# One decoder layer on one core, its instructions put in order by the framework's timeline simulator

## The chip, the core and the metric

The kernel runs on one core of a Trainium2 chip. A core has five engines that work side by side, each through its own list of instructions in a fixed order: TensorE (PE) multiplies matrices and writes PSUM; VectorE (DVE), ScalarE (ACT) and GpSimd (POOL) work on elements; SyncE (SP) here only issues transfers. The engines wait for each other through semaphores. The metric is the device time of one execution in microseconds (us).

## The reference

The layer works on 1024 tokens with 1024 features, all in float32. It is a SwiGLU half step, a mixer of three parallel branches, and a second SwiGLU half step, each between two RMS norms:

```python
f1 = swiglu(rms_norm(h, ffn1_pre_g), ffn1_w_in, ffn1_w_out)      # width 2816
h = h + 0.5 * rms_norm(f1, ffn1_post_g)
u = rms_norm(h, mix_pre_g)
p_rwkv, p_swa, q_mem, gate_logits = split(u @ w_in)
y_a = rwkv7_mix(p_rwkv, ...)              # recurrence over the tokens, 8 heads of 64
y_b = sliding_window_gqa_sinks(...)       # window of 128, 8 query and 2 key heads
y_c = memory_cross_attention(q_mem, ...)  # 256 memory tokens, 4 heads of 128
g_a, g_b, g_c = split(sigmoid(gate_logits + gate_b))
merged = g_a * (y_a @ w_branch[0]) + g_b * (y_b @ w_branch[1]) + g_c * (y_c @ w_branch[2])
h = h + rms_norm(merged @ w_out, mix_post_g)
f2 = swiglu(rms_norm(h, ffn2_pre_g), ffn2_w_in, ffn2_w_out)
h = h + 0.5 * rms_norm(f2, ffn2_post_g)
```

## The kernel before

Features lie on the 128 partitions, tokens along the free axis, in halves of 512. Each large product is made of three matmuls (`mm3`, lines 354 to 356): a value is kept as a rounded part and a remainder (`w_hi`, `w_lo` of a weight; `u` and the like of an input), and the product of the two remainders is left out. A weight tile of 128x512 is loaded by SP into one of 5 buffers `w_raw` (line 269), rounded by ACT into `w_hi` (line 278), and DVE writes the remainder `w_lo` (line 280). There are 8 buffers (`OPS`) for such pairs, so that the pairs are made ahead of the matmuls that use them. Inputs are split in the same way (lines 462 and 463). Both feed-forward stages use a scheme of block products with fewer multiplications, whose sums and differences DVE makes; their parts pass through DRAM (`form_d`, `first_d`, `ffn_sum_d`), stored and loaded by SP (lines 674, 750, 650).

The stages, in order of time: the start (memory keys and values), the first feed-forward stage (to about 700 us), the preparation of the recurrence (`rwkv_prep`, four head pairs, to about 900), the inversion of small triangular matrices on DVE (`rwkv_invert`), beside which PE makes projections, the recurrence in 16 chunks of 64 tokens (`rwkv_chain`, about 1050 to 1155), its norm (`rwkv_finish`), the attention in 16 blocks (`attention`, to about 1460; 8 `MemoryBlock`, 8 `WindowBlock`), the last branch (`last_branches`, to about 1540), the output projection and the second feed-forward stage.

One chunk of the recurrence is a line of small matmuls between which DVE works: `z` (matmul, then a copy, line 1209), its product with the inverse (then two copies to `uv`, line 1218), the new state (a product, then `ts`, line 1227, and `sv`, line 1229), on which the next chunk's `z` waits. Beside it DVE masks the next chunk's gram matrices (`gz`, line 1171), and POOL scales the old state (`sw`, line 1212). Matmuls of two gate projections (`pgate`) are traced behind the chain for PE to use in its waits.

A window block computes scores into PSUM (`sc`, line 94), which ACT and DVE read (lines 127, 128), takes a softmax (line 132 to 142, eight normalisations on line 142), turns the result by PE (`ptr`, line 97), and empties that PSUM bank by ACT (line 152) and DVE (`pt`, line 155). Four PSUM banks serve such tiles (tag `bg`), four others the main products (tag `mm`). In the last branch the gated product is added to the sum by POOL (line 1555).

What sets the order: the Python code is traced once, instruction by instruction, inside a `TileContext`. When the context closes, the framework gives each engine its order. It walks through a simulated execution; where an engine is free, it takes that engine's ready instruction of highest priority. Priority is the traced order, moved forward in blocks under `high_priority(offset=...)` (300 for the weight stream, 1000 for urgent work). Two calls bind the order whatever the simulation says: `keep_in_program_order` puts an instruction behind the one traced before it on its engine (all small matmuls of the recurrence and the attention, and the loads of the start), and `issue_after` puts a group behind a named instruction. For example, the filling of the attention with gate and branch matmuls:

```python
def fill(self, n, behind):
    self.missing += n
    with self.tc.issue_after(behind.ins):
        while self.missing > 0:
            self.missing -= next(self.fills, n)
```

The large matmuls themselves, most of the work of DVE and ACT, and SP's transfers behind the start are free to be placed by the simulated times. The semaphore waits follow from the data and from the order.

Of the kernel before, what the change touches and what calls it, by code (L numbers as in the profile page):

```python
# [1835 lines left out]
def make(arrays):  # L1836
    nc = bacc.Bacc("TRN2", target_bir_lowering=False, num_devices=1, dynamic_dma_scratch_size=SCRATCH)
    io = {}
    for name, a in arrays.items():
        io[name] = nc.dram_tensor(f"in_{name}", a.shape, mybir.dt.from_np(a.dtype), kind="ExternalInput").ap()  # L1840
    io["out"] = nc.dram_tensor("out", [P, KD, T], F32, kind="ExternalOutput").ap()
    with tile.TileContext(nc) as tc:
        Builder(nc, tc, io).build()
    return nc

# [7 lines left out]
```

## Time and profile before

| what | value |
|---|---|
| time, median of 3 runs | 2271.61 us (2271.33 to 2272.18) |
| profiled execution | 2273.16 us |
| its span, first to last instruction | 2271.1 us |
| PE busy | 2244.2 us, 99% of the span |
| weight loads of PE | 1842.2 us, 81% |
| DVE, ACT, POOL busy | 1644.5, 997.3, 80.6 us |
| mean granted PE clock | 0.997 |
| DMA traffic | 417.66 MB, 184 GB/s |

The page of the profile gives busy times, the chain of work that ended last and the costliest groups. A group's row reads: line of the code, engine, operation, output and inputs by their names in the program, shapes, count, busy time, mean duration in ns, and the idle time of the engine before these instructions with what ended it. The waits view has rows of the form "engine, line, waited for: total us, times, longest us". The timeline has the start, the length, the engine and the instruction, with the idle time before it in brackets. SPq and ACTq are the transfers that SP and ACT issue. The granted clock is a share of full speed.

### The profile page before, as it was taken

The page shows a single profiled execution, that of the slowest core. Times are in us where ns is not written, and L with a number is a line of the kernel's source. Part 1 is how long each engine was busy: PE and PEld are TensorE (multiplying, and loading weights), DVE is VectorE, ACT ScalarE, POOL GpSimd, SP SyncE. Part 2 cuts the span into 40 slices and gives each one's busy share as a digit, 9 for nine tenths or more (in the row PEclk, how much of TensorE's full clock was granted, in tenths as well). Part 3 has the DMA queues.
Part 4 walks back from the last instruction along what each step waited for, and adds up shares of the span by engine and source line. Part 5 has one row for each costly group of instructions (what it writes and reads, how often), then busy time and mean ns, then how long its engine had stood idle before and what let it go on. Part 6 is the DMA issues. An engine that isn't in the chain of part 4 may idle for free.

```text
span 2271.1 us, 33412 instructions
## 1 busy us (share of the span) xinstructions
PE 2244.2 (99%) x11868; PEld 1842.2 (81%) x11868; DVE 1644.5 (72%) x2700; ACT 997.3 (44%) x1877; POOL 80.6 (4%) x130
## 2 busy tenths in 40 slices
PE   8999999999999999999999999999999999999998
PEld 6888888888888788888878887778888888888887
DVE  6987767666698885995666576665898885656676
ACT  6533333454555653123444454335663233345451
POOL 0000000000000000001320000031000000000000
PEclk9999999999999999999999999999999999999999
DMA  8465666686654467225438885554465652347763
GB/s 290 156 209 167 219 210 214 209 275 203 193 164 153 116 148 194 105 97 192 146 117 264 289 272 167 201 165 150 158 228 176 193 174 93 114 159 244 216 195 121
DMA packets 280775, 417.66 MB, mean 184 GB/s; under 512 B 82304, under 2 KB 104320, under 8 KB 280352
## 3 DMA queue, kind: packets, MB, share of 16 engines
q1 hardware_dynamic: 272832, 400.26, 55.4%
q10 hardware_dynamic: 7776, 15.28, 2.0%
q8 instruction: 93, 1.52, 0.3%
q14 instruction: 74, 0.61, 0.1%
HBM read 284.89 MB, written 129.50 MB: 182 GB/s over the span
## 4 chain that ended last, share of the span: by engine, by line
PE 90%; DVE 5%; ACT 1%; issue 1%; DMA 1%; POOL 1%; ACTq 0%; SPq 0%; DVEq 0%; POOLq 0%
PE px L354 7%; PE px L356 7%; PE px L355 7%; PE po L355 6%; PE po L354 6%; PE po L356 6%; PE pgate L354 4%; PE pgate L355 4%; PE pgate L356 4%; PE pz L355 3%; PE pz L354 3%; PE pz L356 3%; PE pr L354 2%; PE pr L355 2%; PE pr L356 2%; PE pq L355 1%
## 5 line engine op out<-in xcount | busy, mean ns | idle before, releaser
L278 ACT CAST w_hi<-w_raw 128x512 fp32r<-128x512 f32 x594 | 367.2, 620 | 694.6 <-PE px L355 160.1
L280 DVE TENSOR_TENSOR w_lo<-w_raw,w_hi 128x512 fp32r<-128x512 f32 x594 | 409.2, 690 | 189.2 <-ACT w_hi L278 168.1
L354 PE MATMUL po<-u,w_hi 128*128 128x512 f32 (+1 forms) x476 | 180.9, 380 | 0.0
L356 PE MATMUL po<-u,w_lo 128*128 128x512 f32 (+1 forms) x476 | 180.9, 380 | 0.0
L355 PE MATMUL po<-u,w_hi 128*128 128x512 f32 (+1 forms) x476 | 180.9, 380 | 0.0
L354 PE MATMUL pgate<-u,w_hi 128*128 128x512 f32 x384 | 154.9, 403 | 0.0
L356 PE MATMUL pgate<-u,w_lo 128*128 128x512 f32 x384 | 151.5, 395 | 0.0
L355 PE MATMUL pgate<-u,w_hi 128*128 128x512 f32 x384 | 149.8, 390 | 0.0
L355 PE MATMUL px<-f,w_hi 128*128 128x512 f32 x352 | 137.1, 389 | 0.9 <-DVE f L463 0.9
L354 PE MATMUL px<-u,w_hi 128*128 128x512 f32 x352 | 137.1, 389 | 0.8 <-DVE km L1424 0.8
L354 PE MATMUL px<-f,w_hi 128*128 128x512 f32 x352 | 137.1, 389 | 0.0
L356 PE MATMUL px<-u,w_lo 128*128 128x512 f32 x352 | 137.0, 389 | 0.0
L356 PE MATMUL px<-f,w_lo 128*128 128x512 f32 x352 | 137.0, 389 | 0.0
L355 PE MATMUL px<-u,w_hi 128*128 128x512 f32 x352 | 137.0, 389 | 0.0
L356 PE MATMUL pz<-u,w_lo 128*128 128x512 f32 x352 | 136.9, 389 | 0.0
L354 PE MATMUL pz<-u,w_hi 128*128 128x512 f32 x352 | 136.9, 389 | 0.0
L355 PE MATMUL pz<-u,w_hi 128*128 128x512 f32 x352 | 136.9, 389 | 0.0
L463 DVE TENSOR_TENSOR u<-hid,u 128x512 fp32r<-128x512 f32 x114 | 78.2, 689 | 45.9 <-ACT u L462 45.0
L354 PEld LDWEIGHTS po<-u,w_hi 128*128 128x128 f32 x476 | 89.5, 188 | 17.1
L355 PEld LDWEIGHTS po<-u,w_hi 128*128 128x128 f32 x476 | 89.5, 188 | 17.1
L356 PEld LDWEIGHTS po<-u,w_lo 128*128 128x128 f32 x476 | 89.5, 188 | 16.8
L462 ACT CAST u<-hid 128x512 fp32r<-128x512 f32 x114 | 70.7, 620 | 64.3 <-DMA hid<-form_d 55.1
(397 smaller groups left out, 5111.2 us busy)
## 6 DMA issues: line engine op xcount, KB each, us to landing
w_raw<-in_ffn_in SPq DMA_DIRECT2D x220, 256.0 KB
hid<-form_d SPq DMA_DIRECT2D x154, 256.0 KB
w_raw<-in_win SPq DMA_DIRECT2D x112, 256.0 KB
form_d<-g SPq DMA_DIRECT2D x88, 256.0 KB
w_raw<-ffn_sum_d SPq DMA_DIRECT2D x88, 256.0 KB
form_d<-h SPq DMA_DIRECT2D x66, 256.0 KB
w_raw<-in_ffn_out SPq DMA_DIRECT2D x66, 256.0 KB
gate_d<-gate SPq DMA_DIRECT2D x24, 512.0 KB
```

Of the source, the lines that this page charges most:

```text
L278: self.nc.scalar.copy(hi, x)
L280: self.split_last = self.nc.vector.tensor_tensor(lo, x, hi.bitcast(F32), ALU.subtract)
L354: mm(out, wh, xh, start=first, stop=False, **kw)
L355: mm(out, wh, xl, start=False, stop=False, **kw)
L356: self.last_mm = mm(out, wl, xh, start=False, stop=last, **kw)
L462: self.nc.scalar.copy(hi, x)
L463: self.nc.vector.tensor_tensor(lo, x, hi.bitcast(F32), ALU.subtract)
```

## The change

The context in which the program is traced gets one argument. The framework then walks through the execution with another simulator, which it calls its timeline simulator, when it chooses the order. The traced instructions, their sizes, the buffers, the priorities and the bound orders are the same.

```diff
-    with tile.TileContext(nc) as tc:
+    with tile.TileContext(nc, schedule_with_timeline_sim=True) as tc:
         Builder(nc, tc, io).build()
     return nc
```

## The prediction

> **What bounds the kernel now.** I read the page first: the span, the shares of the engines, and the chain of work that ended last.
>
> ```profile
> span 2271.1 us, 33412 instructions
> ...
> PE 2244.2 (99%) x11868; PEld 1842.2 (81%) x11868; DVE 1644.5 (72%) x2700; ACT 997.3 (44%) x1877; POOL 80.6 (4%) x130
> ...
> PE 90%; DVE 5%; ACT 1%; issue 1%; DMA 1%; POOL 1%; ACTq 0%; SPq 0%; DVEq 0%; POOLq 0%
> ```
>
> TensorE (PE) is busy for 2244.2 of 2271.1 us, and 90% of the chain is its own work. Its idle time is 26.9 us. The change adds and removes no operation, so PE's work stays what it is, and the time can only move through PE's holes: fewer than 26.9 us of them, or more. So the second view is the windows view, cut by stage, which says where the holes are (columns after the window: its length, then busy time and count of PE, weight loads, DVE, ACT, POOL, then granted clock, DMA share and GB/s).
>
> ```profile
> 0.00:20.00 20.00, 13.57 (x53) 11.66 (x54) 9.32 (x20) 12.92 (x22) 0.70 (x6) 1.00 0.91 344
> 100.00:700.00 600.00, 599.96 (x2645) 495.57 (x2644) 445.61 (x722) 258.27 (x443) 2.82 (x15) 1.00 0.63 204
> 700.00:900.00 200.00, 197.82 (x1094) 159.07 (x1093) 163.01 (x188) 107.86 (x167) 4.01 (x16) 1.00 0.55 138
> 900.00:1050.00 150.00, 150.00 (x685) 124.13 (x685) 122.06 (x153) 33.98 (x58) 1.58 (x4) 1.00 0.41 145
> 1050.00:1156.00 106.00, 104.69 (x1915) 87.30 (x1913) 65.13 (x163) 44.40 (x106) 35.08 (x60) 1.00 0.43 128
> 1156.00:1200.00 44.00, 42.95 (x173) 31.89 (x172) 25.17 (x36) 20.10 (x30) 8.50 (x9) 1.00 0.46 156
> 1200.00:1376.00 176.00, 176.00 (x946) 146.74 (x945) 120.17 (x257) 88.11 (x245) 0.96 (x1) 1.00 0.83 272
> 1376.00:1392.00 16.00, 14.70 (x52) 10.68 (x51) 10.21 (x27) 9.21 (x34) 0.00 (x0) 0.79 0.56 186
> 1460.00:1540.00 80.00, 77.52 (x340) 63.24 (x339) 53.48 (x78) 24.11 (x42) 20.68 (x14) 1.00 0.54 179
> 1540.00:2060.00 520.00, 519.64 (x2288) 428.47 (x2286) 382.73 (x607) 226.72 (x395) 3.27 (x2) 1.00 0.50 164
> 2240.00:2271.00 31.00, 21.31 (x176) 20.95 (x175) 17.63 (x49) 5.84 (x16) 2.95 (x4) 0.88 0.33 103
> ```
>
> The two feed-forward stages (100 to 700, 1540 to 2060) have 0.04 and 0.36 us of holes. The start has 6.4 us and the end 9.7 us, together 16.1 of the 26.9. In between lie the small holes of the mixer: 2.2 us in the preparation (700 to 900), 1.3 us in the recurrence (1050 to 1156), 1.05 us behind it, 1.3 us in one block of the attention (1376 to 1392) and 2.5 us in the branches (1460 to 1540), 8.35 us in all.
>
> Is busy PE full PE? Two neighbouring matmuls of a dense stretch start 0.23 us apart:
>
> ```profile
> 1374.42 0.39 PE L354 MATMUL pgate<-u,w_hi 128*128 128x512 f32 x1
> 1374.65 0.39 PE L355 MATMUL pgate<-u,w_hi 128*128 128x512 f32 x1
> ```
>
> In 100 to 700, 2645 matmuls in 600 us are 0.227 us each, so that stage runs at this spacing throughout. [...]
>
> **The change part by part.** No instruction is added, removed or given another size; what may move is each engine's issue order, SP's transfers included. A queue works through its order as written, so what costs is an instruction that stands in front of a more urgent one. I go by stage.
>
> *Feed-forward stages: 0 us.* What could suffer is the stream of weights: load, rounding on ACT, remainder on DVE.
>
> ```profile
> L280 DVE TENSOR_TENSOR w_lo<-w_raw,w_hi 128x512 fp32r<-128x512 f32 x594 | 409.2, 690 | 189.2 <-ACT w_hi L278 168.1
> L278 ACT CAST w_hi<-w_raw 128x512 fp32r<-128x512 f32 x594 | 367.2, 620 | 694.6 <-PE px L355 160.1
> ...
> ACT w_hi L278 <- PE px L355: 176.7, 127, 2.1
> ```
>
> ACT's rounding waits for PE (176.7 us, 127 times) to give back an operand buffer, so the operands are as far ahead as their buffers allow. There are 8 pairs; a pair feeds 12 matmuls of 0.227 us; so the cover is 8 x 12 x 0.227 = 21.8 us (an estimate from the code's 8 and the spacing). An operand costs 0.62 + 0.69 = 1.31 us. A reordering by a few instructions of 0.7 us is lost in 21.8 us. If the cover goes, PE waits for whatever holds the queue; that is the third rival.
>
> *Recurrence: +5.5 us.* It has 16 chunks. One of them, PE's two beginnings and DVE's part between:
>
> ```profile
> 1071.06 0.69 PE L1135 MATMUL z<-sv,gz 128*64 128x64 f32 x16
> ...
> 1076.08 0.48 PE L356 MATMUL pgate<-u,w_lo 128*128 128x512 f32 x1
> ...
> 1077.65 0.69 PE L1135 MATMUL z<-sv,gz 128*64 128x64 f32 x16
> ```
>
> ```profile
> 1075.90 0.41 DVE L1227 TENSOR_TENSOR ts<-z,wc 128x256 f32<-128x256 f32 x1
> 1076.23 0.41 DVE L1171 TENSOR_TENSOR gz<-gram,gmask 128x256 f32<-128x256 f32 x1
> 1076.56 0.86 DVE L1229 TENSOR_TENSOR sv<-ts,sw 64x256 f32<-64x256 f32 x2
> 1077.45 0.43 DVE L1171 TENSOR_TENSOR gz<-gram,gmask 128x256 f32<-128x256 f32 x1
> ```
>
> The chunk takes 1077.65 - 1071.06 = 6.59 us. Its end hangs on the state: `ts`, then `sv`, then the next `z`. One mask of the gram matrix (`gz`) stands between `ts` and `sv` and delays `sv` by 0.33 us; the other comes after. PE fills the wait with gate matmuls from 1076.08 on, 1.4 us of them to the next `z`. Lower bound: the first mask moves behind `sv` too, 15 x 0.33 = -5 us. Upper bound: the second mask also moves ahead of `sv`, 15 x 0.33 = +5 us, and the gate matmuls go too early, twice as many in half of the chunks and none in the rest; then 8 chunks are 1.4 us longer and the 8 others keep their wait as a hole, +11 us; together +16. No row tells which, so I take the middle, +5.5.
>
> *Attention: +11.4 us.* It has 16 blocks, their DVE work in line with the weight remainders. One block shows the price of an unlucky line:
>
> ```profile
> 1378.78 1.66 DVE L142 TENSOR_SCALAR sc<-sc,st 128x128 f32<-128x128 f32 x8
> 1380.35 0.68 DVE L155 TENSOR_TENSOR pt<-ptr,is_own 128x512 f32<-128x512 f32 x1
> 1380.95 0.68 DVE L280 TENSOR_TENSOR w_lo<-w_raw,w_hi 128x512 fp32r<-128x512 f32 x1
> 1381.55 0.68 DVE L155 TENSOR_TENSOR pt<-ptr,is_own 128x512 f32<-128x512 f32 x1
> ```
>
> ```profile
> 1381.09 1.13 PE L94 MATMUL sc<-kd,qs 64*128 64x256 f32 x4 [1.13 <-DVE pt L155]
> 1382.38 1.67 PE L94 MATMUL sc<-kd,qs 64*128 64x256 f32 x4 [0.16 <-DVE pt L155]
> 1383.98 0.79 PE L354 MATMUL pb<-u,w_hi 128*128 128x512 f32 x1
> ...
> 1389.27 0.55 PE L354 MATMUL pb<-u,w_hi 128*128 128x512 f32 x1
> ...
> 1384.00:1389.00 5.00, 5.00 (x13) 3.94 (x13) 2.96 (x5) 0.37 (x1) 0.00 (x0) 0.50 0.84 273
> ```
>
> PE stands for 1.13 + 0.16 = 1.29 us until DVE has emptied the PSUM bank (`pt`, behind eight normalisations and a weight remainder). Then the granted clock is 0.50 from 1384 to 1389: the 12 steps between the matmuls at 1383.98 and 1389.27 take 5.29 us, against 12 x 0.227 = 2.72, so 2.57 us more. One stall costs 1.29 + 2.57 = 3.9 us. I use 3.8, as the slope at its ends is uncertain. Lower bound: this stall goes, -3.8. Upper bound: the other 15 blocks stall too, +57. One block in 16 stalls in the order that stands; with an order that nothing fits to these blocks I take one in four, so three more: +11.4.
>
> [...]
>
> *Preparation: +4.6 us.* Four head pairs, each with a line of wide DVE work.
>
> ```profile
> ACT ep L1022 <- DVE sz L1017: 10.0, 4, 4.3
> ...
> 743.14 2.30 DVE sz L1017
> ```
>
> The widest, a scan of 2.30 us, is waited for in each pair. Lower bound: today's 2.2 us of holes go. Upper: in each pair such an instruction stands before the one that PE needs, 4 x 2.3 = +9.2. I take half, since DVE has 163 of 200 us filled here and an unlucky place is as likely as a harmless one.
>
> *Behind the recurrence and the branches: +2.5 us.* Holes today: 1.05 + 2.48 = 3.5 us, which may go (-3.5). In the branches each merged sum passes through POOL:
>
> ```profile
> L1555 POOL TENSOR_TENSOR u<-u,gin 128x512 f32<-128x512 f32 x16 | 24.0, 1505 | 309.3 <-DVE gin L1553 309.3
> ```
>
> If all 16 came to stand on the path, +24 us. The next projection needs them only when it reaches them, so I stay near the low end: the branches' hole doubles, +2.5.
>
> *Start and end: 0 us.* The transfers and matmuls of the start are kept in traced order by the code, and the end is one chain of data; nothing there is a choice of order. 900 to 1050 has no hole, with the inversion on DVE (122 of 150 us); the operand cover hides it.
>
> **Sum.** 5.5 + 11.4 + 4.6 + 2.5 = 24.0 us. The profiled execution took 2273.16 us (span 2271.1 and 2.1 us around it), 1.55 us above the median of the runs, 2271.61. So 2297 for such an execution, and 2271.61 + 24.0 = 2296 for the median. The lower bounds add to -5 - 3.8 - 2.2 - 3.5 = -14.5 (2257), the upper ones to 16 + 57 + 9.2 + 24 = +106 (2378).
>
> **Rivals.**
> *Faster.* The first mask moves behind `sv` in every chunk and the block at 1381 loses its stall: -5 - 3.8 = -8.8, 2263 us. It decides as soon as more is won in these two places than 4.5 us. For it: both are plain flaws of an order. Against it: the mixer's holes hold 8.35 us in all, and everything else there is full already. Chance 0.08.
> *No change.* The order differs only under the cover of 21.8 us and in engines that have slack (DVE 72%, ACT 44%), or the two orders are nearly one. Then 2272 us, within 0.2% (4.5 us), which is about what a measurement of this kernel can tell from none. For it: 1120 of 2271 us are feed-forward stages without holes, and much of the mixer's order is written out in the code. Chance 0.14.
> *Much slower, by SP's queue.* All weight loads and most stores go through one queue.
>
> ```profile
> SPq L269 <- DVE w_lo L280: 892.0, 484, 9.8
> ...
> SPq L674 <- DVE g L734: 33.8, 22, 3.4
> ```
>
> Today a store waits 3.4 us at most for its data, 22 times, with weight loads behind it. If the new order puts the store more than 21.8 us ahead of its data, the operands run dry. At 5 us beyond the cover in each of the 22 groups, +110 us, 2382. Against it: that is over six times today's longest wait. Chance 0.13.
>
> **How the numbers follow.** The forecast, slower by 5 to 75 us, has the remaining 0.65; its value is 2296. Slower is 0.65 + 0.13 = 0.78, same 0.14, faster 0.08. The range reaches to the faster rival below and nearly to the queue's below its full price: 2264 to 2375.
>
> **What would show it.** The counts of instructions (PE 11868) and their mean times stay. PE's idle grows beyond 26.9 us, and in the mixer, while the feed-forward windows stay full. The recurrence's chunk is longer than 6.59 us, or its gate matmuls sit elsewhere. More attention windows have a clock below 1.00, each behind a short wait for `pt` or a score bank. It is wrong if the holes lie in the feed-forward stages behind `w_hi` and DMA (the queue), or if the mixer's holes are below 8.35 us.

## The result: slower by 2.8%, and the profile after

The changed kernel takes 2334.86 us (median of 4 runs, 2332.17 to 2339.24), the kernel before on the same chip 2271.89 us (4 runs). The ratio is 1.0278, with a 95% interval of 1.0266 to 1.0290. The forecast was 2296 us: the direction was right, the time lies inside the range, but the loss is 63 us where 24 were forecast.

The profiled execution took 2339.24 us. From the page of the changed kernel:

```profile
span 2337.5 us, 33359 instructions
...
PE 2261.3 (97%) x11868; PEld 1853.6 (79%) x11868; DVE 1661.5 (71%) x2700; ACT 997.9 (43%) x1879; POOL 83.3 (4%) x130
...
PE 87%; DVE 6%; DMA 3%; ACT 2%; issue 2%; SPq 0%; DVEq 0%; POOL 0%; ACTq 0%
```

PE, DVE and POOL do as many instructions as before, ACT two more (1879 against 1877). The span is 66.4 us longer, and PE accounts for all of it: its idle time is 2337.5 - 2261.3 = 76.2 us against 26.9, which is +49.3, and its busy time grew by 17.1 us with the same 11868 matmuls. The mean granted clock fell from 0.997 to 0.990; that alone is 2337.5 x 0.010 - 2271.1 x 0.003 = 16.6 us (an estimate from the two rounded means), so the busy time grew mostly because some matmuls ran at a lower clock. So the loss is holes in PE and what follows a hole. The windows view of the changed kernel says where they are (columns as in the prediction; the difference of the first two numbers after the window is the hole):

```profile
0.00:20.00 20.00, 13.30 (x49) 11.27 (x50) 9.13 (x20) 13.04 (x23) 0.70 (x6) 1.00 0.89 322
20.00:130.00 110.00, 104.20 (x417) 79.71 (x416) 87.55 (x152) 57.60 (x103) 0.00 (x0) 0.95 0.55 184
130.00:400.00 270.00, 270.00 (x1193) 223.58 (x1192) 198.98 (x317) 89.96 (x158) 0.00 (x0) 1.00 0.60 197
400.00:500.00 100.00, 94.28 (x412) 76.71 (x411) 70.55 (x126) 41.11 (x75) 3.10 (x15) 1.00 0.73 242
720.00:750.00 30.00, 24.63 (x104) 19.96 (x102) 19.73 (x30) 13.87 (x25) 1.12 (x2) 0.94 0.34 114
750.00:1100.00 350.00, 350.00 (x1932) 284.21 (x1930) 273.12 (x328) 135.02 (x216) 7.15 (x22) 1.00 0.50 140
1100.00:1203.00 103.00, 79.14 (x1637) 68.17 (x1634) 56.72 (x142) 35.90 (x87) 31.82 (x55) 0.95 0.34 102
1203.00:1460.00 257.00, 250.95 (x1258) 201.65 (x1257) 163.67 (x343) 126.52 (x326) 9.55 (x10) 0.99 0.72 233
1460.00:1660.00 200.00, 197.83 (x917) 160.70 (x916) 136.81 (x210) 82.18 (x166) 26.96 (x16) 1.00 0.51 168
1660.00:1700.00 40.00, 34.45 (x141) 27.66 (x140) 29.27 (x45) 25.11 (x45) 0.00 (x0) 0.91 0.34 110
1755.00:1780.00 25.00, 20.50 (x73) 13.98 (x73) 23.52 (x40) 13.19 (x23) 0.00 (x0) 0.93 0.38 127
1780.00:2300.00 520.00, 520.00 (x2322) 431.74 (x2321) 367.75 (x580) 209.92 (x363) 0.00 (x0) 1.00 0.55 176
2300.00:2337.50 37.50, 27.02 (x223) 26.54 (x221) 18.96 (x51) 6.26 (x17) 2.90 (x4) 0.90 0.27 85
```

Two kinds of place lost. The recurrence (1100 to 1203) has 23.9 us of holes, against 1.3 before. And the joints around and inside the feed-forward stages, where one product ends and the next waits for its input (20 to 130, 400 to 500, 720 to 750, 1660 to 1700, 1755 to 1780), have 5.8 + 5.7 + 5.4 + 5.6 + 4.5 = 27.0 us. In the kernel before, about the same places (20 to 130, 390 to 480, 700 to 740, 1605 to 1720) have 2.5 us. The long dense stretches, 130 to 400 and 1780 to 2300, have none, nor have 500 to 720 and 1700 to 1755, which the view above leaves out, and neither has the preparation and inversion (750 to 1100).

**The recurrence.** PE's first matmuls of three neighbouring chunks and, in the second fence, DVE's part between two of them, from the timeline of the changed kernel (start, length, instruction, and in brackets the idle time before it and what ended it):

```profile
1139.80 0.69 PE L1135 MATMUL z<-sv,gz 128*64 128x64 f32 x16 [1.78 <-DVE sv L1229]
1146.84 0.69 PE L1135 MATMUL z<-sv,gz 128*64 128x64 f32 x16 [1.79 <-DVE sv L1229]
1153.84 0.69 PE L1135 MATMUL z<-sv,gz 128*64 128x64 f32 x16 [1.75 <-DVE sv L1229]
```

```profile
1143.84 1.52 DVE L1171 TENSOR_TENSOR gz<-gram,gmask 64x256 f32<-64x256 f32 x4 [0.84 <-PE gram L1135]
1145.29 0.41 DVE L1227 TENSOR_TENSOR ts<-z,wc 128x256 f32<-128x256 f32 x1
1145.82 0.87 DVE L1229 TENSOR_TENSOR sv<-ts,sw 64x256 f32<-64x256 f32 x2
```

A chunk takes 7.04 us, where it took 6.59, and 1.78 us of it is a hole. Two things changed. DVE makes all four masks (`x4`) ahead of `ts` and `sv`, where two stood ahead, one between them and one behind. And PE has no gate matmuls left for the wait: they all stand ahead of 1103 us, 22 at the head of the stage and 50 and 17 in the first two chunks, which take 15.6 and 9.6 us without a hole. The chunks behind them have none, where the kernel before has six or more in each.

**The joints.** At the end of the first feed-forward stage, PE's side (timeline of the changed kernel), and under it the rounding that its first two rows read:

```profile
729.39 0.39 PE L449 MATMUL ps_rs<-sq_hi,mean_r 128*128 128x512 f32 x1
730.29 0.39 PE L449 MATMUL ps_rs<-sq_lo,mean_r 128*128 128x512 f32 x1
736.50 2.08 PE L354 MATMUL pr<-u,w_hi 128*128 128x512 f32 x4 [5.37 <-ACT u L462]
```

```profile
724.38 0.73 ACT L443 ACTIVATE sq_hi<-sq,eps 128x512 fp32r<-128x512 f32 x1 [1.42 <-DVE sq L476]
```

The norm's two mean matmuls (line 449) are ready by about 726 us, but stand on PE's queue behind matmuls of a query projection until 729.39 and 730.29. When they are done, two matmuls of that filling are left, and PE stands 5.37 us until the norm's chain has made `u`. In the kernel before, the same matmuls start as soon as the rounding is there, 49 matmuls of the query projection come behind the second one, and `pr` follows without a hole:

```profile
703.92 0.50 PE L449 MATMUL ps_rs<-sq_hi,mean_r 128*128 128x512 f32 x1 [0.37 <-ACT sq_hi L443]
...
716.18 0.39 PE L354 MATMUL pr<-u,w_hi 128*128 128x512 f32 x1
```

At the head of the second feed-forward stage PE waits for DVE (timeline of the changed kernel, DVE's rows, then PE's):

```profile
1676.53 2.08 DVE L516 SCALAR_TENSOR_TENSOR acc<-acc,vecs,rs 128x512 f32<-128x512 f32 x3
1678.52 0.68 DVE L280 TENSOR_TENSOR w_lo<-w_raw,w_hi 128x512 fp32r<-128x512 f32 x1
1679.12 3.40 DVE L516 SCALAR_TENSOR_TENSOR acc<-acc,vecs,rs 128x512 f32<-128x512 f32 x5
1682.43 0.68 DVE L463 TENSOR_TENSOR u<-acc,u 128x512 fp32r<-128x512 f32 x1
```

```profile
1683.17 0.79 PE L355 MATMUL px<-u,w_hi 128*128 128x512 f32 x1 [4.00 <-DVE u L463]
```

Eight scalings stand ahead of the first remainder of an input, and PE waits 4.00 us for it. The kernel before has the eight scalings ahead too (line 516, from 1616.05 to 1622.56 us), so DVE's order is not what is new there. What is new is again the filling. In the kernel before the norm's mean matmuls started at 1610.40 and 1611.20, and the last matmul of the output projection (`pw`) at 1625.36, so that projection covered the chain:

```profile
1610.40 0.50 PE L449 MATMUL ps_rs<-sq_hi,mean_r 128*128 128x512 f32 x1
...
1625.36 0.39 PE L356 MATMUL pw<-u,w_lo 128*128 128x512 f32 x1
```

In the changed kernel they start at 1671.28 and 1672.18, and the last `pw` at 1676.04: the filling ends some 10 us sooner after the norm.

### The profile page after: what moved, and what is told of

Same layout as the page of the kernel before. It is cut to its first block, busy times and chain, and to the rows that moved or that the text cites. A ratio compares the mean times of both kernels' runs of the same rounds, so it can differ in the third digit from the quotient of the medians.

```text
span 2337.5 us, 33359 instructions
## 1 busy us (share of the span) xinstructions
PE 2261.3 (97%) x11868; PEld 1853.6 (79%) x11868; DVE 1661.5 (71%) x2700; ACT 997.9 (43%) x1879; POOL 83.3 (4%) x130
## 4 chain that ended last, share of the span: by engine, by line
PE 87%; DVE 6%; DMA 3%; ACT 2%; issue 2%; SPq 0%; DVEq 0%; POOL 0%; ACTq 0%
PE px L354 7%; PE px L356 7%; PE px L355 7%; PE po L356 6%; PE po L355 6%; PE po L354 6%; PE pz L354 3%; PE pz L356 3%; PE pz L355 3%; PE pgate L354 3%; PE pgate L355 3%; PE pgate L356 3%; PE pr L354 2%; PE pr L356 2%; PE pr L355 2%; PE pb L355 2%
## 5 line engine op out<-in xcount | busy, mean ns | idle before, releaser
L355 PEld LDWEIGHTS po<-u,w_hi 128*128 128x128 f32 x476 | 89.5, 188 | 17.1
L354 PEld LDWEIGHTS po<-u,w_hi 128*128 128x128 f32 x476 | 89.5, 188 | 17.1
```

The costliest lines, as they stand in the source:

```text
L354: mm(out, wh, xh, start=first, stop=False, **kw)
L355: mm(out, wh, xl, start=False, stop=False, **kw)
```

## The experiments

All of them use one method. The program is traced twice. The first trace gives the order in which one of the two simulators puts each engine's instructions; in the second trace, chosen instructions of chosen engines are bound to that order, and the simulator places the rest.

```diff
+def order(nc):
+    body = max(nc.cur_f.blocks, key=lambda b: len(b.instructions))
+    return {e: [i.name for i in body.instructions if i.engine == t] for e, t in ENGINES.items()}
+
+def bound(orders):
+    def bind(nc, tc, b):
+        traced = {i.name: i for i in nc.cur_bb.bb.instructions}
+        for names in orders:
+            names = [n for n in names if n in traced]
+            for a, c in zip(names, names[1:]):
+                tc.add_manual_dep(traced[c], a, mybir.DependencyInfo(mybir.DependencyClass.NoSync, ...), reason="order")
+    return bind
```

Names that begin with t_ start from the changed kernel and take something back; names that begin with d_ start from the kernel before and take something over. The runs come from several chips, so each is compared with runs of the kernel before on its own chip, and I give its excess: (ratio - 1) x 2271.6 us. The changed kernel's excess is 63.2 us (60.4 to 65.9).

**Which engine's order?** Theories: Q, PE's own order spends its filling too early; D, the orders of DVE and ACT make PE's inputs late; S, SP's queue (the third rival). Each kernel binds one engine over the whole program; for t_PE the edit is the following, for t_DVE and t_SP the name differs, and d_PE takes `order(trace(arrays, True))` and traces with `False`.

```diff
 def make(arrays):
-    ...
+    default = order(trace(arrays, False))
+    return trace(arrays, True, bound([default["PE"]]))
```

t_PE, the changed kernel with PE in the order of before:

> The order of the kernel after, but with PE's instructions bound to the order they have in the kernel before; DVE, ACT, POOL and SP are still ordered by the timeline simulator. Theory Q (PE's own order is the cause: in the trace after, its filling matmuls go ahead of small matmuls on which others wait, and are used up before the waits that they should cover): most of the 63 us comes back, 2275 to 2295 us, and the recurrence's 13 holes of 1.8 us are gone. Theory D (the operands and results made by DVE and ACT come late): 2320 to 2335 us. Theory S (SP's queue): 2320 to 2335 us.

t_DVE, the same with DVE:

> The order of the kernel after, but with DVE's instructions bound to the order they have in the kernel before; the other engines are ordered by the timeline simulator. Theory Q: 2315 to 2335 us, at most the four masks ahead of the state in each chunk (13 x 0.45 = 6 us) come back. Theory D: 2275 to 2300 us. Theory S: no change, 2325 to 2340 us.

t_SP, the same with SP:

> The order of the kernel after, but with SP's transfers bound to the order they have in the kernel before. Theory Q and theory D: no change, 2325 to 2340 us. Theory S: 2275 to 2305 us.

d_PE, the kernel before with PE in the changed kernel's order:

> The kernel before, but with PE's instructions bound to the order they have in the kernel after; the other engines are ordered by the default simulator, which sees PE's order. Theory Q: 2320 to 2340 us, the recurrence again with holes of 1.8 us. Theory D and theory S: 2272 to 2290 us.

Measured:

| kernel | median us | ratio to before (95%) | excess us |
|---|---|---|---|
| t_PE | 2312.93 | 1.0185 (1.0165 to 1.0204) | 42.0 |
| t_DVE | 2322.50 | 1.0229 (1.0211 to 1.0248) | 52.0 |
| t_SP | 2347.75 | 1.0344 (1.0323 to 1.0365) | 78.1 |
| d_PE | 2310.98 | 1.0174 (1.0156 to 1.0192) | 39.5 |

Theory S falls: with SP's old order the kernel is 15 us slower still. PE's order alone costs 39.5 us in the kernel before, yet taking it back leaves 42.0 us. The two numbers add to 81.5, more than the 63.2 that there are, so PE's order and the orders of the other engines cost partly the same time. My reading is that where PE has nothing to do, it matters less that its input is late. Q and D both miss t_PE and d_PE, which lie between their ranges; only t_DVE lies where a theory, Q, had it. None of the three engines tried is the cause alone (ACT and POOL were not tried by themselves), and the question was put by stage instead.

**Which stage?** Theory A: each stage's order costs what it costs by itself, and the costs add. Theory B: a hole in one stage is made up in another. Marks set during the trace cut out the instructions of a stage, and all five engines, or PE alone, are bound to the order of before within it (`traced` lists the instructions as they were traced, `full` holds each engine's order in the kernel before):

```diff
+    inside = set(traced[MARKS["chain"]:MARKS["finish"]])      # t_chain, t_chainPE; t_ffn1: traced[0:MARKS["mixer"]]; t_ffn2: traced[MARKS["branches"]:]
+    bound([[n for n in full[e] if n in inside] for e in ('PE', 'DVE', 'ACT', 'POOL', 'SP')])(nc, tc, b)      # t_chainPE: ('PE',)
```

t_ffn1, all that is traced ahead of the mixer in the order of before:

> The order of the kernel after, but all that is traced before the mixer (the start, the first feed-forward stage, the hand-over with its norms and the first projections) bound on all five engines to the order of the kernel before. Theory A (each stage has its own loss, so stages add up): the lag when the recurrence begins is 22 us in the traces (1048.6 against 1070.7), so 2335 - 22 = 2313 us. Theory B (what one stage loses is partly lost time that a later stage would have had to wait anyway): at least 8 us less comes back, above 2321 us.

t_chain, the recurrence and the two gate projections traced with it:

> The order of the kernel after, but the recurrence and the two gate projections traced behind it bound on all engines to the order of the kernel before. In the traces the recurrence takes 107.1 us before and 132.2 us after. Theory A: 2335 - 25 = 2310 us, chunks of 6.6 us without holes. Theory B: above 2318 us.

t_chainPE, the same on PE alone:

> As the run that binds the recurrence on all engines, but PE alone bound there. Theory Q (PE spends the gate matmuls too early): about 19 of the 25 us come back, 2316 us, and the chunk stays 0.4 us longer for the masks that DVE puts ahead of the state. If DVE's order is what makes the holes: 2330 us or more.

t_ffn2, all that is traced from the last branches on:

> The order of the kernel after, but all that is traced behind the attention (last branch, output projection, second feed-forward stage) bound on all engines to the order of the kernel before. The lag grows from 48.8 us at the last gated sum to 65.6 us at the last norm in the traces. Theory A: 2335 - 17 = 2318 us. Theory B: above 2326 us.

t_three binds these three stages at once:

> The changed kernel, with the two feed-forward stages and the recurrence in the order of before on all engines; free are the preparation, the inversion, the attention and the first branches. Theory A: 15.8 + 16.6 + 24 to 32 us come back, 2270 to 2279 us, and the rest of the mixer cost less than 8 us. By the prediction's terms for the attention, the preparation and the branches (11.4 + 4.6 + 2.5) it would be about 2290 us.

Measured (given back: the changed kernel's excess less this one's, before rounding):

| kernel | median us | ratio to before (95%) | excess us | given back us |
|---|---|---|---|---|
| t_ffn1 | 2319.09 | 1.0215 (1.0200 to 1.0230) | 48.8 | 14.3 |
| t_chain | 2302.89 | 1.0144 (1.0129 to 1.0159) | 32.7 | 30.4 |
| t_ffn2 | 2318.25 | 1.0214 (1.0199 to 1.0229) | 48.6 | 14.5 |
| t_three | 2275.75 | 1.0025 (1.0016 to 1.0035) | 5.7 | 57.5 |
| t_chainPE | 2315.21 | 1.0202 (1.0185 to 1.0219) | 45.9 | 17.3 |

The first three rows add to 59.3 us, and all three together give back 57.5, which is the same within their intervals of 3 to 4 us each: theory A holds for the sum. t_ffn1 by itself lies between the two theories: 14.3 us came back where A had 22, a lag read from the traces. What is left, 5.7 us (3.6 to 8.0), is what the preparation, the inversion, the attention and the first branches cost; it also bounds what the binding itself may add, as no run binds a kernel to its own order. In t_chain the recurrence is full again, as the windows view shows:

```profile
1066.00:1171.00 105.00, 104.49 (x1924) 87.36 (x1924) 65.68 (x163) 44.91 (x106) 34.98 (x59) 1.00 0.43 135
```

**The recurrence taken apart.** Two suspects: gate matmuls spent early (PE), and masks ahead of the state (DVE). d_chain takes the changed kernel's whole recurrence over into the kernel before, d_chainPE only PE's order of it, d_chainDVE only DVE's:

```diff
+    full = order(trace(arrays, True))
+    inside = set(traced[MARKS["chain"]:MARKS["finish"]])
+    bound([[n for n in full[e] if n in inside] for e in ('PE', 'DVE', 'ACT', 'POOL', 'SP')])(nc, tc, b)      # ('PE',), ('DVE',)
+    return trace(arrays, False, bind)
```

> The kernel before, with the recurrence alone (and the two gate projections traced with it) in the changed kernel's order on all engines. Theory A, the stages' orders cost what they cost by themselves and add: +25 to +32 us, 2295 to 2302 us, with the same holes of 1.8 us ahead of the z matmuls in some 13 chunks. Theory B, the recurrence's order costs that only behind the changed kernel's later arrival and its other queues: under +10 us.

> The kernel before, with PE alone in the changed kernel's order in the recurrence: its gate matmuls come in the first three chunks, DVE keeps one mask ahead of the state and one behind it in nearly all chunks. The hole of 1.78 us is then 0.33 us shorter: 13 x 1.45 = +19 us, about 2289 us, if the filling spent early is the main part. If the masks carry the cost, under +6 us.

> The kernel before, with DVE alone in the changed kernel's order in the recurrence: both masks ahead of the state in every chunk, six gate matmuls per chunk on PE as before. The state comes 0.33 us later in 15 chunks: +5 us, about 2275 us, if PE's six gate matmuls (1.4 us) do not cover it. Over +12 us would mean that DVE's order carries the recurrence's loss.

d_state goes the other way and tries the prediction's lower bound in the kernel before:

```diff
                 for q in (0, 1):
-                    V.tensor_tensor(nxt["sv"][ROWS[q], q], t[ROWS[q]], sw[ROWS[q]], ALU.add)
-                masked(nxt, 1)
+                    state = V.tensor_tensor(nxt["sv"][ROWS[q], q], t[ROWS[q]], sw[ROWS[q]], ALU.add)
+                with self.tc.issue_after(state.ins):
+                    masked(nxt, 1)
```

> The kernel before, with both masks of the second half of the gram matrix behind the state sv on DVE. By the prediction's lower bound each chunk's state comes 0.33 us sooner: -5 us, 2265 us, faster than both kernels. The rival: PE has 1.3 us of holes in the whole recurrence, so a state that comes sooner only moves gate matmuls to another place: 0 to -1.3 us, 2270 to 2272 us.

| kernel | median us | ratio to before (95%) | excess us |
|---|---|---|---|
| d_chain | 2294.43 | 1.0106 (1.0091 to 1.0122) | 24.1 |
| d_chainPE | 2286.92 | 1.0073 (1.0058 to 1.0088) | 16.6 |
| d_chainDVE | 2291.12 | 1.0096 (1.0079 to 1.0113) | 21.8 |
| d_state | 2272.92 | 1.0013 (1.0004 to 1.0022) | 3.0 |

d_chain alone brings 24.1 us (20.7 to 27.7), which agrees with theory A's 25 to 32 only at its lower end. The waits view (engine, line, waited for: total us, times, longest) parts it. First d_chain, then d_chainPE, then t_chainPE, in which the gate matmuls sit as before and only the masks are the changed kernel's:

```profile
PE z L1135 <- DVE sv L1229: 23.1, 13, 1.8
```

```profile
PE z L1135 <- DVE sv L1229: 16.3, 13, 1.3
```

```profile
PE z L1135 <- DVE sv L1229: 7.0, 15, 0.8
```

Gate matmuls spent early leave 13 holes of 1.25 us, 16.3 us. Masks ahead of the state leave 15 holes of 0.47 us, 7.0 us, beside six gate matmuls per chunk. Together that is 23.3, and d_chain, which has both, waits 23.1. A chunk of d_chainPE, from its timeline (PE's rows, then DVE's):

```profile
1110.45 0.69 PE L1135 MATMUL z<-sv,gz 128*64 128x64 f32 x16 [1.24 <-DVE sv L1229]
1116.96 0.69 PE L1135 MATMUL z<-sv,gz 128*64 128x64 f32 x16 [1.26 <-DVE sv L1229]
```

```profile
1115.29 0.41 DVE L1227 TENSOR_TENSOR ts<-z,wc 128x256 f32<-128x256 f32 x1
1115.62 0.41 DVE L1171 TENSOR_TENSOR gz<-gram,gmask 128x256 f32<-128x256 f32 x1
1115.95 0.86 DVE L1229 TENSOR_TENSOR sv<-ts,sw 64x256 f32<-64x256 f32 x2
```

With no filling at all the chunk takes 1116.96 - 1110.45 = 6.51 us. With its six gate matmuls it took 6.59 in the kernel before. So the filling is nearly free where it sits in the wait, and costs its full 1.3 us per chunk where it does not: the chain through DVE is hardly shortened by taking it away. The second mask lengthens it from 6.51 to 7.04 us, by 0.53, where the prediction had 0.33.

d_chainDVE missed its expectation, and for a reason that the expectation had wrong: with DVE bound, the simulator also moved PE's gate matmuls into the first five chunks (11 holes of `z` in its waits, 17.9 us), so it repeats d_chain more than it isolates the masks. The price of the masks is taken from t_chainPE instead.

d_state's state comes sooner, and the kernel gains nothing; it is 3.0 us above before (0.9 to 5.0). The lower bound falls, and the rival's reading holds: PE had 1.3 us of holes in the whole stage, so there was nothing to win. What is new in its waits view is as large as its loss: a chunk takes 6.4 us in place of 6.59, but with four gate matmuls in place of six and a short hole at its end.

```profile
PE z L1135 <- DVE sv L1229: 3.1, 15, 0.3
```

No kernel of this study beats the kernel before.

**The joints taken apart.** The same two theories, Q and D, for the 28.8 us of the two feed-forward stages. t_ffnPE binds PE alone in both, t_ffnAD binds DVE and ACT alone in both, and t_norm binds DVE and ACT in the norms and activation factors only:

```diff
+    inside = set(traced[:MARKS["mixer"]] + traced[MARKS["branches"]:])      # t_norm: the instructions of pre_norm, factors_norm, factors_first, factors_part, factors_end
+    bound([[n for n in full[e] if n in inside] for e in ('PE',)])(nc, tc, b)      # t_ffnAD, t_norm: ('DVE', 'ACT')
```

> The changed kernel, with PE alone in the order of before in the two feed-forward stages (all that is traced ahead of the mixer and from the last branches on). The same stages on all engines gave back 15.8 and 16.6 us. Theory Q, it is PE's own order that spends the filling of the hand-overs too early: most of the 32 us comes back, 2335 - 25 to 32 = 2303 to 2310 us. Theory D, it is the order of DVE and ACT in the norms of the hand-overs: at most 8 us, 2327 us or more.

> The changed kernel, with DVE and ACT alone, and of these only the instructions of the norms and of the activation factors ahead of the three big stages, in the order of before among themselves. Theory D: the hole behind the second norm of the mixer's end (1683 us, where DVE does eight scalings of acc before the first remainder of u) goes, and with it 10 us or more, 2325 us or less. Theory Q: the holes stay, since the norm's matmuls still stand behind filling on PE's queue, within 5 us of 2335 us.

> The changed kernel, with DVE and ACT alone in the order of before in the two feed-forward stages. If these two engines carry the stages' loss: 20 us or more come back, 2315 us or less. If it is the fit of all engines' orders that counts, no set of engines alone gives the 32 us back: 3 to 12 us, 2323 to 2332 us.

| kernel | median us | ratio to before (95%) | excess us | given back us |
|---|---|---|---|---|
| t_ffnPE | 2329.61 | 1.0255 (1.0239 to 1.0272) | 57.9 | 5.2 |
| t_norm | 2329.25 | 1.0255 (1.0241 to 1.0269) | 57.9 | 5.2 |
| t_ffnAD | 2339.20 | 1.0304 (1.0288 to 1.0319) | 69.1 | -5.9 |

Both theories missed. Theory Q had 25 to 32 us for PE's order, and it gives back 5, where D had at most 8. But theory D had 10 us or more for t_norm and 20 or more for t_ffnAD; the one gives back 5, the other nothing, and t_norm leaves both large waits in place (4.6 us for the first `pr`, 4.0 for `px` at the second stage). The waits view tells why. First t_ffnPE, then t_ffnAD:

```profile
PE ps_rs L449 <- ACT sq_hi L443: 7.1, 5, 1.8
...
PE px L354 <- DVE u L708: 6.5, 4, 3.4
PE px L354 <- ACT w_hi L278: 3.3, 1, 3.3
```

```profile
PE pr L354 <- ACT u L462: 5.8, 1, 5.8
PE px L355 <- DVE u L463: 3.6, 2, 3.1
PE po L355 <- DVE u L463: 3.5, 2, 1.8
```

With PE's old order the wait for `u` behind the norm is gone, but the mean matmuls now stand at the head of PE's queue and wait for a rounding that ACT makes late: 7.1 us that the changed kernel did not have. With the old order on DVE and ACT, PE's filling is spent as early as in the changed kernel, and its waits stay. I read this so: an order of one engine fits the orders of the others that were made with it. What the runs show is that on all engines the same two stages give back 28.8 us, and on PE, or on DVE and ACT, 5 at most. Whether PE, DVE and ACT together would do without POOL and SP was not tried.

## Why the prediction was right and where it failed

The direction came true and the size did not: 63 us where 24.0 were forecast. Two terms of the sum failed, the feed-forward stages, put at 0 us and measured at 28.8, and the recurrence, put at 5.5 and measured at 24.1 to 30.4. Of the 24.0 us, 18.5 stood in stages that together cost 5.7, so that the sum came as near as it did is partly luck.

*What bounds the kernel* was right: PE's counts stayed, and the time moved through PE's holes, +49.3 us. One item was priced for the stalls of the attention alone: PE's busy time grew by 17.1 us, mostly at a lower clock, and that lay behind the holes of the other stages too (the clock is 0.95 from 1100 to 1203 and 0.91 from 1660 to 1700).

*Recurrence, +5.5 us.* Both mechanisms of the upper bound occurred: the second mask moved ahead of the state, and the gate matmuls went too early. The term is mis-sized: 24.1 us, more than the upper bound of 16. The step that failed is "twice as many in half of the chunks and none in the rest": all of them were spent at the head of the stage and in its first two chunks, so 13 chunks have the wait as a hole, and their loss is 16.3 us where the bound allowed 11. The masks cost 7.0 us where it allowed 5. Taking the middle of two bounds was no estimate either; the lower one was never to be had, since a stage with 1.3 us of holes cannot win 5 (d_state).

*Feed-forward stages, 0 us.* This failed for the joints. The cover argument held for what it was about: the stream of weights runs dry in no dense stretch, and 130 to 400 and 1780 to 2300 have no hole. But it was applied to whole stages from windows that averaged over them, and the windows shown leave out 20 to 100 us, where the kernel before has 1.7 us of its holes, 0.9 of them in front of a product with `f`. At the joints the wait is for activations, a norm's chain of eight or more instructions over ACT, DVE and PE, and its cover is filling that one order saves up and another spends. That cost 28.8 us, about as much as the recurrence (30.4 by the same measure), and the sign that these windows stay full failed (5.7 us from 400 to 500).

*Attention, +11.4 us.* Too high. Holes from 1203 to 1460 are 6.1 us, against 1.05 + 1.30 behind the recurrence and in the attention before; all that is left free in t_three, the attention among it, costs 5.7 us. One long stall for `pt` is in the changed kernel (2.5 us) in place of the one of before (1.29 us); there were not three more.

*Preparation, +4.6, and branches, +2.5.* Neither came. 750 to 1100 has no hole, where the preparation had 2.2 us, and 1460 to 1660 has 2.2 us, where the branches had 2.5.

*Start and end, 0 us.* Right: holes of 6.7 and 10.5 us, against 6.4 and 9.7.

*Rivals.* The faster one had its room in two flaws of the order of before. The mask turned out to be worth nothing (d_state); the stall at 1381 us was not tried by itself. The queue of SP is refuted as the cause by t_SP, and by its own rows in the changed kernel's waits:

```profile
SPq L269 <- DVE w_lo L280: 731.7, 387, 24.4
...
SPq L869 <- DVE acc L867: 54.9, 21, 27.0
```

Its condition did occur once: a store (line 869) waited 27.0 us for its data, longer than the cover of 21.8; the 24.4 us are a load's wait for its buffer. But its price did not: in PE's waits a rounded weight is named once in the whole changed kernel, with 1.7 us. The rival's reading of before was too narrow as well. The 3.4 us are the longest wait in the one row that it shows; in the same view of the kernel before a store of line 1297 waits 13.0 us and one of line 869 already 22.5 us, and the feed-forward windows were full all the same. I take it that a long wait of the queue hurts only where the operands behind it are needed soon; no run tests this.

What stays open: taking the recurrence back gives 30.4 us in the changed kernel, putting it into the kernel before costs 24.1; the intervals (27.1 to 33.9, without the changed kernel's own, and 20.7 to 27.7) hardly meet, and no run tells where the rest comes from. The clock may be a part of it: in the profiled runs PE ran at half clock for 10.2 us in the changed kernel's recurrence (from 1125.1 and 1196.8 us), and in d_chain the clock from 1160 to 1200 was 0.96, which is 0.04 x 40 / 0.5 = 3.2 us at half clock (an estimate from the rounded 0.96), but one profile of each shows no more than that. What in the joints belongs to which engine is open too, and so is why the timeline simulator chose this order.

## What to carry to other kernels

Independent matmuls that an engine can do at any time are a store. Where a chain through other engines leaves a fixed wait per step, it pays to ration them: here an order that issued them as soon as they were ready spent them in the first two of 16 steps and left the later waits as holes, 16.3 us. Before costing a change of order at nothing, look at the joints between stages by narrow windows, since an average over a dense stage hides them. And do not expect much from mending one engine's order alone: here it won back at most 21 of 63 us, and whole stages bound on all engines won back 57.5.

## What the runs showed of the hardware

A hole can cost more than its length. After 2.78 us of idle time at the head of the first feed-forward stage of the changed kernel (timeline), the matmuls that follow start 0.43 us apart, where the prediction's rows show 0.23; the granted clock is 0.50 from 101.1 to 107.9 us (windows view):

```profile
101.72 0.80 PE L354 MATMUL px<-f,w_hi 128*128 128x512 f32 x1 [2.78 <-DVE u L708]
102.31 0.63 PE L355 MATMUL px<-f,w_hi 128*128 128x512 f32 x1
102.74 0.63 PE L356 MATMUL px<-f,w_lo 128*128 128x512 f32 x1
```

But equal holes do not cost the same. Of the 13 holes of 1.75 to 1.79 us that end between 1110 and 1196.1, two were followed by slower matmuls. The chunk behind the first took 8.44 us in place of 7.04; behind the second, ahead of the last chunk at 1196.04, a group of 16 matmuls took 1.12 us in place of 0.68:

```profile
1124.32 0.86 PE L1135 MATMUL z<-sv,gz 128*64 128x64 f32 x16 [1.77 <-DVE sv L1229]
...
1132.76 0.69 PE L1135 MATMUL z<-sv,gz 128*64 128x64 f32 x16 [1.77 <-DVE sv L1229]
...
1197.37 1.12 PE L1135 MATMUL y<-f,sv 64*64 64x64 f32 x16
```

I had expected every stall to bring the clock down, as the one in the attention before did (0.50 from 1384 to 1389 us). In the changed kernel the two drops in the recurrence begin at 1125.1 and 1196.8 us, 0.8 us after the end of a hole of 1.77 and of 1.79 us. The clock records in its trace have eight stretches at half clock ahead of the kernel's end, from 39.7, 101.1, 736.0, 1125.1, 1196.8, 1418.6, 1681.5 and 1770.2 us; they last 3.41 or 6.83 us each, and their starts lie whole multiples of 3.413 us apart. In the 3.4 us ahead of the two drops in the recurrence PE was busy for 1.63 and 1.61 us of 3.40. Six other stretches of that length, from 1108.0, 1114.9, 1166.1, 1172.9, 1179.7 and 1186.5 us, had 1.61 to 1.65 us and no drop followed, so the busy share alone does not decide it; what does, the trace does not show.
